# Output projection by Strassen's seven half-size products, with weight sums made in DRAM by accumulating transfers

## The chip, the cores and the metric

The kernel runs on one core of one Trainium2 chip. The metric is device time in microseconds (us) of one execution, as the median of several. PE is TensorE (its weight loads are a row of their own, PEld), DVE is VectorE, ACT is ScalarE, POOL is GpSimd, and SP is SyncE, which here only issues transfers.

## The reference

One layer of a decoder: one input projection, three branches (a gated MLP, a state-space scan, attention into 256 memory tokens), a concatenation `y` of 1024 columns, and then the part that the change rewrites:

```python
y = jnp.concatenate([y_a * jax.nn.silu(g_a), y_b * jax.nn.silu(g_b), y_x * jax.nn.silu(g_x)], axis=-1)
x = layer_norm(DN_ALPHA * x + y @ w_out[layer], ln_g[layer], ln_b[layer])
```

There are 1024 tokens, 1024 columns of `y` and 1024 columns of output, all float32; `DN_ALPHA` is the fourth root of 2.

## The kernel before

All matrix products keep float32 accuracy by three matmuls: every operand is split into a high part, rounded to the float32r that PE takes, and a low part that holds the rest. `split` (L64) makes them, a cast on ACT (L65) and a subtraction on DVE (L62), and `mm3` (L142) multiplies high by high, high by low and low by high. A tile of weights is 128 x 512: `load` (L130) brings 256 KB into one of four `raw` buffers, on SP's queue, and `piece` (L135) splits it into one of six `hi`/`lo` pairs.

The program runs through these stages, all back to back on PE: eight k-steps of the first projections (`gx`, `q`; x and its weights are loaded and split on the way; each k-step is 24 matmuls), the keys and values of the memory (`k`, `v`; pieces `wk`, `wv`, with `qs` made from `q` at the same time by `q_evac`, L256), the units `xb`, `gb`, `v`, `u`, `g` of the input projection with attention and the scan woven in, and the output projection `o`.

PE's order is the order of the code. `ordered` (L107) says whether DVE, ACT and POOL are bound to it too ("a": in the first k-steps and from the third `g` unit on) or whether a planner places their instructions ("p": between). SP's transfers are always placed by the planner. Small jobs (`spawn`, `tick`) are written into the code's order by a count of PE's time.

The output projection (L905 to L1017) goes through the 1024 output columns in two halves. In the first, eight banks of PSUM hold eight token tiles of 128, and the eight k-steps run outside, tiles inside; `o_part` (L961) adds `ALPHA * x`, which is in `res`, while it evacuates, and takes batch statistics. In the second half, tiles run outside: as one tile is complete, `finish_a` (L939) aggregates its statistics, lets POOL raise the variance to the power -1/2 (L943) and centres it on DVE (L944); `finish_b` (L947) scales on ACT (L951), adds the bias on POOL (L59) and stores it, or, for the last three tiles, does both on DVE in cuts (L957). The last tile's second half is done in two pieces of 256 columns.

Also touched: `token_bias` (L637), which starts the attention stage and has POOL fill a tile `ones` (L647) that a matmul `tb` (L650) needs.

## Time and profile before

| | |
|---|---|
| median of 3 runs | 388.81 us (388.75 to 390.43) |
| the profiled execution | 388.28 us, span 386.5 us |
| PE busy | 377.0 us, 98% of the span |
| DVE, ACT, POOL busy | 273.7, 155.6, 97.6 us |
| moved by the transfers | 37.95 MB |

The span runs from the first to the last instruction of the profiled execution. Busy times are unions over an engine's instructions, so a pipelined PE can be busy without a gap. A chain of waits is followed back from the last instruction. In a timeline, a bracket behind a row gives the idle time of the engine before it and what ended it. SPq rows are the issues of transfers by SP. Buffer numbers are left out of names.

### The profile page before, as it was taken

The numbers are of one execution on the slowest core, as the hardware profiler recorded it, in microseconds if no ns is written. First come the engines' busy times: TensorE is split into PE (matmuls) and PEld (weight loads), VectorE is DVE, ScalarE is ACT, GpSimd is POOL, SyncE is SP. The second block draws the span as 40 slices with busy tenths as digits, with TensorE's granted clock in tenths as the row PEclk, the third lists the DMA queues.
The fourth block names the chain that finished last, engine by engine and source line by source line (L and its number), as shares of the span: only waits on it lengthen the run. The fifth ranks groups of instructions, "written<-read, shape, count | busy, mean of one in ns | idle before, by whom it ended". The sixth has DMA issues, their size and how long they took to land.

```text
span 386.5 us, 5465 instructions
## 1 busy us (share of the span) xinstructions
PE 377.0 (98%) x1937; PEld 319.9 (83%) x1937; DVE 273.7 (71%) x589; ACT 155.6 (40%) x305; POOL 97.6 (25%) x77
## 2 busy tenths in 40 slices
PE   8999999999999999999999999999999999999991
PEld 7888898888888788888888888888888888888881
DVE  4689997888884999699677387958247401874476
ACT  4572696667673735131232334337136410012200
POOL 1305000000000885814927402200000000027761
PEclk9999999999999999999999999999999999999997
DMA  7973436312940123112111144000038710001224
GB/s 219 301 266 117 137 113 190 116 71 77 105 66 30 30 70 110 54 30 69 56 44 54 39 114 161 33 0 27 29 109 336 280 37 0 2 0 58 107 109 163
DMA packets 23339, 37.95 MB, mean 98 GB/s; under 512 B 5504, under 2 KB 8976, under 8 KB 23184
## 3 DMA queue, kind: packets, MB, share of 16 engines
q1 hardware_dynamic: 23312, 37.61, 31.9%
q8 instruction: 15, 0.25, 0.3%
q14 instruction: 12, 0.10, 0.1%
HBM read 31.77 MB, written 5.24 MB: 96 GB/s over the span
## 4 chain that ended last, share of the span: by engine, by line
PE 94%; issue 1%; ACT 1%; DVE 1%; DMA 1%; POOLq 0%; POOL 0%; SPq 0%; DVEq 0%
PE o L145 7%; PE o L146 7%; PE o L144 7%; PE zu L151 4%; PE zu L152 4%; PE zg L151 4%; PE zu L154 4%; PE zg L152 4%; PE zg L154 4%; PE zv L144 4%; PE zv L146 4%; PE zv L145 4%; PE av L624 2%; PE zxb L152 2%; PE zxb L154 2%; PE zxb L151 2%
## 5 line engine op out<-in xcount | busy, mean ns | idle before, releaser
L943 POOL TENSOR_TENSOR stat<-stat,nhalf 128x1 f32<-128x1 f32 x8 | 12.1, 1510 | 112.3 <-DVE stat L942 112.3
L145 PE MATMUL o<-l_wo,yh 128*128 128x512 f32 (+1 forms) x100 | 38.4, 384 | 0.0
L144 PE MATMUL o<-h_wo,yh 128*128 128x512 f32 (+1 forms) x100 | 38.3, 383 | 0.0
L146 PE MATMUL o<-h_wo,yl 128*128 128x512 f32 (+1 forms) x100 | 38.3, 383 | 0.0
L144 PE MATMUL zv<-h_v,xh 128*128 128x512 f32 x64 | 25.6, 400 | 0.3 <-ACT yb L229 0.3
L151 PE MATMUL zu<-xh,h_u 128*128 128x512 f32 x64 | 25.9, 404 | 0.0
L151 PE MATMUL zg<-xh,h_g 128*128 128x512 f32 x64 | 25.5, 398 | 0.0
L152 PE MATMUL zu<-xl,h_u 128*128 128x512 f32 x64 | 25.0, 391 | 0.0
L152 PE MATMUL zg<-xl,h_g 128*128 128x512 f32 x64 | 25.0, 390 | 0.0
L146 PE MATMUL zv<-h_v,xl 128*128 128x512 f32 x64 | 24.9, 390 | 0.0
L145 PE MATMUL zv<-l_v,xh 128*128 128x512 f32 x64 | 24.9, 389 | 0.0
L962 DVE SCALAR_TENSOR_TENSOR res<-res,o 128x512 f32<-128x512 f32 (+1 forms) x16 | 10.3, 646 | 19.0 <-PE o L146 19.0
L144 PEld LDWEIGHTS o<-h_wo,yh 128*128 128x128 f32 x100 | 18.8, 188 | 3.9
L145 PEld LDWEIGHTS o<-l_wo,yh 128*128 128x128 f32 x100 | 18.8, 188 | 3.9
L146 PEld LDWEIGHTS o<-h_wo,yl 128*128 128x128 f32 x100 | 18.8, 188 | 3.8
L62 DVE TENSOR_TENSOR l_v<-r_v,h_v 128x512 fp32r<-128x512 f32 x16 | 15.6, 978 | 7.2 <-ACT h_v L65 7.1
L65 ACT CAST h_v<-r_v 128x512 fp32r<-128x512 f32 x16 | 9.9, 620 | 26.4 <-PE zu L152 18.4
L951 ACT ACTIVATE res<-res,stat 128x1024 f32<-128x1024 f32 x5 | 5.8, 1152 | 36.6 <-POOL stat L943 36.6
L154 PE MATMUL zu<-xh,l_u 128*128 128x512 f32 x64 | 19.8, 390 | 0.0
L154 PE MATMUL zg<-xh,l_g 128*128 128x512 f32 x64 | 19.7, 389 | 0.0
L596 ACT ACTIVATE pr<-s,nm 128x256 f32<-128x256 f32 x32 | 14.9, 472 | 7.9 <-DVE nm L592 6.5
L62 DVE TENSOR_TENSOR l_wo<-r_wo,h_wo 128x512 fp32r<-128x512 f32 x12 | 8.0, 689 | 14.0 <-ACT h_wo L65 13.9
(296 smaller groups left out, 1068.6 us busy)
## 6 DMA issues: line engine op xcount, KB each, us to landing
r_v<-in_w_v_dram SPq DMA_DIRECT2D x16, 256.0 KB, 2.8
r_wo<-in_w_o_dram SPq DMA_DIRECT2D x16, 256.0 KB, 2.9
res<-in_x_dram SPq DMA_DIRECT2D x8, 512.0 KB, 6.6
r_x<-in_xT_dram SPq DMA_DIRECT2D x15, 256.0 KB, 4.8
out_dram<-res SPq DMA_DIRECT2D x6, 512.0 KB, 2.6
r_u<-in_w_fm_dram SPq DMA_DIRECT2D x8, 256.0 KB, 2.7
r_g<-in_w_fm_dram SPq DMA_DIRECT2D x8, 256.0 KB, 2.7
r_wgq<-in_w_gq_dram SPq DMA_DIRECT2D x7, 256.0 KB, 4.9
```

The source lines that it names most:

```text
L62: eng.tensor_tensor(o, a, b, op=ALU.subtract)
L65: S.copy(hi, src)
L144: T.matmul(ps, lhsT=sh, rhs=mh, start=start, stop=False, **kw)
L145: T.matmul(ps, lhsT=sh, rhs=ml, start=False, stop=False, **kw)
L146: T.matmul(ps, lhsT=sl, rhs=mh, start=False, stop=stop, **kw)
L151: T.matmul(ps[h], lhsT=wh, rhs=xh[:, kt, half[h]], start=first, stop=False, **kw[h])
L152: T.matmul(ps[h], lhsT=wh, rhs=xl[:, kt, half[h]], start=False, stop=False, **kw[h])
L154: T.matmul(ps[h], lhsT=wl, rhs=xh[:, kt, half[h]], start=False, stop=last, **kw[h])
L596: S.activation(pr[:, h], ps3[:, h], AF.Exp, bias=nm[:, h:h + 1], scale=1.0, accum_out=rs[:, h:h + 1])
L624: T.matmul(ps[:, h * 256:h * 256 + 256], lhsT=vs[:, m, 2 * hp + h], rhs=pp[:, h * 2 + m], start=h + m + n == 0, stop=h + m + n == 3, skip_ ...
L943: G.tensor_tensor(rs, rs, nhalf[:, 0:1], op=ALU.pow)
L962: V.scalar_tensor_tensor(res[:, t, c0:c0 + w], res[:, t, c0:c0 + w], ALPHA, ps[:, :w], op0=ALU.mult, op1=ALU.add)
```

## The change

The 1024 x 1024 x 1024 product becomes seven products of 512 x 512 x 512 after Strassen, in Winograd's form. Tokens are cut in halves h1 and h2, the columns of `y` in the halves (`yx`, `yb`) and `ya`, and the weights in quarters a11, a12, a21, a22. Four weight sums s1 to s4 are tensors in DRAM: SP copies a quarter into each, and POOL's queue adds the others by accumulating transfers. When they are loaded like other weights, twelve of the pieces (of s2, s4 and s3) get their low part differently: ACT casts the high part and writes its negative as the low part, and an accumulating transfer from DRAM adds the weights to it. Operands of `y` that are sums (T1 to T4) are made on DVE and then split; four of them are made in place in `yx` and `yb`.

Products run in the order of the code's list of weights (a11, s1, s2, s4, s3, a22, a12), five of them with the four k-steps outside and four token tiles inside, and the last two, T4 times a22 and B21 times a12, tile by tile. Products that share a sum stay in the same PSUM banks (`ub`, `zb`) and are evacuated in between. Layer norm no longer takes batch statistics, except for the last tile: the evacuations also add up their rows, ACT squares with the mean as bias and adds up (`means`), POOL takes the power (`deviations`), DVE centres, and `finish` scales and adds.

```diff
+    def weight_sums():
+        yield 4.0
+        nc.sync.dma_start(out=wsum["s1"], in_=quarter["a21"])
+        nc.sync.dma_start(out=wsum["s3"], in_=quarter["a21"])
+        yield 16.0
+        G.dma_start(out=wsum["s1"], in_=quarter["a22"], accum_op=ALU.add)
+        G.dma_start(out=wsum["s3"], in_=quarter["a11"], accum_op=ALU.add)
+        nc.sync.dma_start(out=wsum["s2"], in_=quarter["a11"])
+        yield 16.0
+        G.dma_start(out=wsum["s2"], in_=wsum["s1"], accum_op=ALU.add,
+                      max_dma_last_dim=8192)
+        nc.sync.dma_start(out=wsum["s4"], in_=quarter["a12"])
+        yield 16.0
+        G.dma_start(out=wsum["s4"], in_=wsum["s2"], accum_op=ALU.add,
+                      max_dma_last_dim=8192)
+
     spawn(token_bias())
+    spawn(weight_sums())
...
+    def differences(k):
+
+        b12, b11 = src1(k)[:, h2], src1(k)[:, h1]
+        sub(V, b12, ya[:, k, h2], b12)
+        V.scalar_tensor_tensor(b11, b11, -1.0, b12, op0=ALU.mult, op1=ALU.subtract)
...
+                if 8 <= i < 20:
+                    S.copy(hi, self.raws[i])
+                    S.activation(lo, hi.bitcast(F32), AF.Copy, scale=-1.0)
+                    G.dma_start(out=lo, in_=self.src(i), accum_op=ALU.add)
+                else:
+                    split(hi, lo, self.raws[i])
...
+    wo = Weights(("a11", "s1", "s2", "s4", "s3", "a22", "a12"))
...
+    def means(t0, n):
+        i = slice(at(t0), at(t0) + n)
+        V.tensor_tensor(nmean[:, i], sums[:, i, 0], sums[:, i, 1], op=ALU.add)
+        V.tensor_scalar(nmean[:, i], nmean[:, i], -1.0 / 1024, None, op0=ALU.mult)
+        for t in range(t0, t0 + n):
+            junk = gm.tile([P, 1024], BF16, tag="mt", bufs=2, name=f"junk{t}")
+            i1 = slice(at(t), at(t) + 1)
+            S.activation(junk, res[:, t], AF.Square, bias=nmean[:, i1], scale=1.0,
+                         accum_out=ssq[:, i1])
+
+    def deviations(t0, n):
+        i = slice(at(t0), at(t0) + n)
+        V.tensor_scalar(rsd[:, i], ssq[:, i], 1.0 / 1024, LN_EPS, op0=ALU.mult, op1=ALU.add)
+        G.tensor_tensor(rsd[:, i], rsd[:, i], nhalf[:, 0:n], op=ALU.pow)
...
+    def finish(t, cuts=None):
+        rs = rsd[:, at(t):at(t) + 1]
         ot = res[:, t]
-        if t < 5:
+        if cuts is None:
             S.activation(ot, ot, AF.Copy, scale=rs)
             add(G, ot, ot, lnb2)
             nc.sync.dma_start(out=out[tok[t]], in_=ot)
             return
...
+    def product(p, n, ps, start, done):
+        for k in range(4):
+            wo.fetch(4 * p + k + 5)
+            for j in range(4):
+                omm(ps[j], n, k, 4 * p + k, j, start and k == 0, k == 3)
+                if k == 3:
+                    done(j)
+                tick(0.68)
...
+    product(0, "B11", ub, True, lambda j: first(j, 0, ub[j], 1))
+    product(1, "T1", zb, True, lambda j: first(4 + j, 1, zb[j], -1))
+    product(2, "T2", ub, False, lambda j: first(4 + j, 0, ub[j], 1))
+    product(3, "B22", zb, False, lambda j: more(4 + j, 0, zb[j], 1, True))
+
+    def t2_done(j):
+        more(4 + j, 1, ub[j], -1, True)
+        if j < 2:
+            means(4 + j, 1)
+
+    product(4, "T3", ub, False, t2_done)
+    drain()
+    wo.fetch(28)
+    means(6, 2)
+    deviations(4, 2)
...
+    def last(j):
+        p2(j)
+        more(j, 0, z2[j], 1, True)
+        means(j, 1)
+
+    p4(0)
+    centre(4)
+    first(0, 1, ub[0], -1, True)
+    deviations(6, 2)
+    centre(5)
+    last(0)
+    finish(4)
+    centre(6)
+    deviations(0, 1)
+    centre(0)
+    p4(1)
+    first(1, 1, ub[1], -1, True)
+    finish(5)
+    last(1)
+    finish(0)
+    centre(7)
+    deviations(1, 1)
+    centre(1)
+    p4(2)
+    first(2, 1, ub[2], -1, True)
+    finish(6, (0, 1024))
+    last(2)
+    finish(1)
+    finish(7, (0, 1024))
+    deviations(2, 1)
+    centre(2)
+    p4(3)
+    first(3, 1, ub[3], -1)
+    V.bn_stats(bst[:, 0], res[:, 3, half[1]])
+    finish(2)
```

Three places show how instructions stand now. First SP's queue at the end of the first k-steps' loads; `ws` are the four sums, `gluw` a parameter, and the `r_m`, `r_wgq` and `r_x` behind them are the loads for the last k-step. The piece of the difference:

```order
 L639 DMA gluw<-in_glu_w_dram 128x512
+L664 DMA ws_s_819<-in_w_o_dram 128x2048
+L665 DMA ws_s_821<-in_w_o_dram 128x2048
+L669 DMA ws_s_820<-in_w_o_dram 128x2048
+L673 DMA ws_s_822<-in_w_o_dram 128x2048
 L132 DMA r_m_520<-in_memT_dram 128x512
 L132 DMA r_wgq_524<-in_w_gq_dram 128x512
```

The planner has put all four copies ahead of the last k-step's loads, long before the stage in which the code asks for them. On POOL, the four accumulating transfers stand behind the power `rr` (L417) and a fill, and ahead of the fill of `ones`.

Second, DVE in the stage of keys and values, before:

```order
L62 TENSOR_TENSOR l_wv_622<-r_wv_619,h_wv_621 128x512
L62 TENSOR_TENSOR l_wk_685<-r_wk_682,h_wk_684 128x512
L264 SCALAR_TENSOR_TENSOR qs<-q_161,qs 64x512 x2
L264 SCALAR_TENSOR_TENSOR qs<-q_162,qs 64x512 x2
L62 TENSOR_TENSOR l_wv_691<-r_wv_688,h_wv_690 128x512
L264 SCALAR_TENSOR_TENSOR qs<-q_163,qs 64x512 x2
L264 SCALAR_TENSOR_TENSOR qs<-q_164,qs 64x512 x2
```

And now, at the same place:

```order
L62 TENSOR_TENSOR l_wv_622<-r_wv_619,h_wv_621 128x512
L264 SCALAR_TENSOR_TENSOR qs<-q_161,qs 64x512 x2
L264 SCALAR_TENSOR_TENSOR qs<-q_162,qs 64x512 x2
L264 SCALAR_TENSOR_TENSOR qs<-q_163,qs 64x512 x2
L264 SCALAR_TENSOR_TENSOR qs<-q_164,qs 64x512 x2
L62 TENSOR_TENSOR l_wk_685<-r_wk_682,h_wk_684 128x512
L62 TENSOR_TENSOR l_wv_691<-r_wv_688,h_wv_690 128x512
```

The low parts of the third pair of pieces (`l_wk_685`, `l_wv_691`) moved behind all of `qs`; on ACT their casts moved behind its `qs` and a table load in the same way.

Third, POOL's last instructions now; `stat` rows are powers of the variance, `res` rows whole-tile adds of the bias:

```order
L1046 TENSOR_TENSOR stat<-stat,nhalf 128x2 x2
L59 TENSOR_TENSOR res<-res,lnp 128x1024
L1046 TENSOR_TENSOR stat<-stat,nhalf 128x1
L59 TENSOR_TENSOR res<-res,lnp 128x1024 x2
L1046 TENSOR_TENSOR stat<-stat,nhalf 128x1
L59 TENSOR_TENSOR res<-res,lnp 128x1024
L1046 TENSOR_TENSOR stat<-stat,nhalf 128x1
L59 TENSOR_TENSOR res<-res,lnp 128x1024
L1202 TENSOR_TENSOR stat<-stat,nhalf 128x1
```

In before, adds and powers alternate and the last two powers follow each other; now tile 2's add stands directly ahead of the last tile's power.

## Rows read from the trace of the kernel before

**Rows 1.** The page: busy us and share of the span; shares of the chain.

```profile
PE 377.0 (98%) x1937; PEld 319.9 (83%) x1937; DVE 273.7 (71%) x589; ACT 155.6 (40%) x305; POOL 97.6 (25%) x77
...
PE 94%; issue 1%; ACT 1%; DVE 1%; DMA 1%; POOLq 0%; POOL 0%; SPq 0%; DVEq 0%
```

**Rows 2.** Timeline of PE: start us, us, engine, line, operation, out<-in; output projection's ends.

```profile
289.92 0.40 PE L144 MATMUL o<-h_wo,yh 128*128 128x512 f32 x1
...
378.18 0.28 PE L146 MATMUL o<-h_wo,yl 128*128 128x256 f32 x1
```

**Rows 3.** Groups of PE by form, 289.8 to 378.6: count | busy us, mean ns.

```profile
L145 PE MATMUL o<-l_wo,yh 128*128 128x512 f32 x92 | 36.1, 392 | 0.0
...
L145 PE MATMUL o<-wb_l,yh 128*128 128x512 f32 x28 | 11.0, 392 | 0.0
L145 PE MATMUL o<-l_wo,yh 128*128 128x256 f32 x8 | 2.3, 282 | 0.0
```

**Rows 4.** Timeline of DVE, its last row.

```profile
382.06 1.54 DVE L957 SCALAR_TENSOR_TENSOR res<-res,stat,lnp 128x480 f32<-128x480 f32 x3 [0.44 <-POOL stat L943]
```

**Rows 5.** Timeline of POOL near the end: an add, and the last power.

```profile
365.22 2.40 POOL L59 TENSOR_TENSOR res<-res,lnp 128x1024 f32<-128x1024 f32 x1
...
380.50 1.52 POOL L943 TENSOR_TENSOR stat<-stat,nhalf 128x1 f32<-128x1 f32 x1 [4.25 <-DVE stat L942]
```

**Rows 6.** The page: a group of splits; a transfer's KB and us to landing.

```profile
L62 DVE TENSOR_TENSOR l_wo<-r_wo,h_wo 128x512 fp32r<-128x512 f32 x12 | 8.0, 689 | 14.0 <-ACT h_wo L65 13.9
...
r_wo<-in_w_o_dram SPq DMA_DIRECT2D x16, 256.0 KB, 2.9
```

**Rows 7.** Timeline of ACT: the scale of a whole tile.

```profile
365.28 1.15 ACT L951 ACTIVATE res<-res,stat 128x1024 f32<-128x1024 f32 x1 [4.35 <-POOL stat L943]
```

**Rows 8.** Timeline of SP: issues at the end of the first k-steps' loads.

```profile
23.43 0.33 SPq L639 DMA_DIRECT2D gluw<-in_glu_w_dram  x1
...
27.93 0.93 SPq L132 DMA_DIRECT2D r_x<-in_xT_dram  x2
```

**Rows 9.** Windows: load phase; loads of x and weights; a store of a tile.

```profile
23.00:26.00 3.00, 3.00 (x15) 2.49 (x14) 2.51 (x14) 2.28 (x4) 0.46 (x1) 1.00 1.00 353
26.00:28.00 2.00, 2.00 (x11) 1.65 (x10) 1.99 (x4) 1.91 (x4) 0.00 (x0) 1.00 0.26 92
...
300.00:304.00 4.00, 4.00 (x19) 3.23 (x18) 0.00 (x0) 0.50 (x1) 0.00 (x0) 1.00 1.03 403
352.00:353.25 1.25, 1.25 (x7) 1.05 (x6) 1.18 (x4) 0.00 (x0) 0.52 (x1) 1.00 1.01 413
```

**Rows 10.** Timeline of PE: eighth k-step's first matmul, third wk piece's, the ones'.

```profile
43.34 0.39 PE L151 MATMUL gx<-xh,h_wgq 128*128 128x512 f32 x1
...
54.48 0.28 PE L144 MATMUL k<-mh,h_wk 128*128 128x256 f32 x1
...
70.72 1.02 PE L650 MATMUL tb<-wT,ones 128*128 128x512 f32 x2
```

**Rows 11.** Timeline of DVE: eighth k-step's last two splits; the first of two qs runs.

```profile
40.46 1.28 DVE L62 TENSOR_TENSOR xl<-r_x,xh 128x512 fp32r<-128x512 f32 x2
...
49.78 2.80 DVE L264 SCALAR_TENSOR_TENSOR qs<-q,qs 64x512 fp32r<-64x512 f32 x4 [0.23 <-ACT qs L261]
```

**Rows 12.** Timeline of POOL between 22 and 66 us.

```profile
29.10 5.44 POOL L417 TENSOR_TENSOR rr<-et,EE 128x32 f32<-128x32 f32 x1 [5.64 <-DVE th L56]
...
60.51 0.21 POOL L647 MEMSET ones<- 128x128 f32 x1 [25.90 <-ACT h_xb L65]
```

**Rows 13.** Timeline of ACT: the table load behind qs.

```profile
53.95 1.28 ACT L237 ACT_TABLE_LOAD   x1
```

**Rows 14.** Windows behind PE's end; the granted clock is the third number from the end.

```profile
379.00:381.00 2.00, 0.00 (x0) 0.00 (x0) 1.90 (x6) 0.00 (x0) 0.50 (x1) 1.00 0.79 297
381.00:382.00 1.00, 0.00 (x0) 0.00 (x0) 0.62 (x1) 0.00 (x0) 1.00 (x1) 0.68 0.00 0
```

**Rows 15.** Timeline of PE at the start: the warm-up matmuls.

```profile
1.08 3.17 PE L243 MATMUL warm<-warm 128*128 128x128 bf16 x28 [1.08 <-DVE warm L240]
```

More of the change, by code (lines that the diff above doesn't have):

```diff
@@ L906, in trunk_kernel @@
     yp1_st, yp1 = open_pool("yp1", side="right")
[L907 to L919 removed]
+    h1, h2 = half
@@ new lines, in src1, with block, ysplit @@
+    def src1(k):
+        return (yx if k < 2 else yb)[:, k % 2]
+    ops = {}
+    def block(n, k, pool, tag):
+        t = [pool.tile([P, 512], F32R, tag=f"{tag}{x}", bufs=8 if tag == "y1" else 7, name=f"{n}{x}{k}") for x in "hl"]
+        ops[n, k] = t
+        return t
+    def ysplit(n, k, src, pool, tag):
+        split(*block(n, k, pool, tag), src)
+    def early_split():
+        for k in range(4):
+            ysplit("B11", k, src1(k)[:, h1], yp1, "y1")
+            yield 2.0
+        for k in range(4):
+            t = gm.tile([P, 512], F32, tag="mt", bufs=2, name=f"T1f{k}")
+            sub(V, t, src1(k)[:, h1], src1(k)[:, h2])
+            ysplit("T1", k, t, yp1, "y1")
+            yield 3.0
+        for k in range(3):
+            while k not in have_y:
+                yield 1.0
+            differences(k)
+            yield 2.0
@@ L1008, in trunk_kernel, with first @@
-    for c in range(2):
-        ps = zbank(f"o17{c}")
-        for i in range(KT):
-            wh, wl = wo1[i]
-            omm(ps[:, :256], 7, i, wh[:, c * 256:c * 256 + 256], wl[:, c * 256:c * 256 + 256])
-        o_part(7, 512 + c * 256, 256, ps, 2 + c)
-        if c == 0:
-            finish_b(6)
-    finish_a(7, 4)
-    finish_b(7)
+    def first(t, c, ps, sign, total=False):
+        r = res[:, t, half[c]]
+        kw = dict(accum_out=sums[:, at(t), c:c + 1]) if total else {}
+        V.scalar_tensor_tensor(r, r, ALPHA, ps, op0=ALU.mult,
+                               op1=ALU.add if sign > 0 else ALU.subtract, **kw)
@@ new lines, in more, with yprep @@
+    def more(t, c, ps, sign, total=False, cols=(0, 512)):
+        a, b = cols
+        r = res[:, t, 512 * c + a:512 * c + b]
+        kw = dict(accum_out=sums[:, at(t), c:c + 1]) if total else {}
+        V.scalar_tensor_tensor(r, ps[:, a:b], float(sign), r, op0=ALU.mult, op1=ALU.add, **kw)
+    ub = [ubank(f"o1{j}") for j in range(4)]
+    zb = [zbank(f"o5{j}") for j in range(4)]
+    def yprep():
+        differences(3)
+        for k in range(4):
+            ysplit("T2", k, src1(k)[:, h1], yp, "y2")
+            yield 2.0
+        for k in range(3):
+            ysplit("B22", k, ya[:, k, h2], yp, "y2")
+            yield 2.0
+        yield 2.0
+        for k in range(4):
+            ysplit("T3", k, src1(k)[:, h2], yp1, "y1")
+            yield 2.0
+        yield 3.0
+        ysplit("B22", 3, ya[:, 3, h2], yp, "y2")
+        yield 2.0
+        for k in range(4):
+            t4 = src1(k)[:, h1]
+            V.scalar_tensor_tensor(t4, t4, -1.0, ya[:, k, h1], op0=ALU.mult, op1=ALU.subtract)
+            ysplit("T4", k, t4, yp1, "y1")
+            yield 2.0
+        for k in range(4):
+            ysplit("B21", k, ya[:, k, h1], yp, "y2")
+            yield 2.0
@@ new lines, in omm @@
+    def omm(ps, n, k, w, j, start, stop, cols=(0, 512)):
+        wh, wl = wo.pcs[w]
+        a, b = cols
+        yh, yl = ops[n, k]
+        mm3(ps[:, a:b], yh[:, tok[j]], yl[:, tok[j]], wh[:, a:b], wl[:, a:b], start, stop, chk=True)
+    def product(p, n, ps, start, done):
+        for k in range(4):
+            wo.fetch(4 * p + k + 5)
[4 more added lines that the diff above has]
+                tick(0.68)
@@ new lines, in p2 @@
+    def p2(j, first=True, cols=(0, 512)):
+        for k in range(4):
+            omm(z2[j], "B21", k, 24 + k, j, first and k == 0, k == 3, cols)
+    def last(j):
[17 more added lines that the diff above has]
+    finish(0)
@@ new lines, in trunk_kernel @@
+    centre(7)
[13 more added lines that the diff above has]
+    finish(2)
+    for c, cols in enumerate(((0, 256), (256, 512))):
+        p2(3, c == 0, cols)
+        more(3, 0, z2[3], 1, False, cols)
+        V.bn_stats(bst[:, 1 + c], res[:, 3, cols[0]:cols[1]])
```

133 lines of the change are left out of this document (63 added, 70 removed).

## The prediction

> **What bounds the kernel now.** I read the busy shares and the chain that ended last first: TensorE (PE) is busy 98% of the span and carries 94% of the chain [rows 1]. So PE work that goes is worth its full length, and so is any wait put on PE. Then the stage that the change rewrites: its first matmul starts at 289.92 and its last ends at 378.18 + 0.28 = 378.46 [rows 2], 88.5 us without a hole. Grouped by form, one of the three lines of mm3 holds 92 + 28 matmuls of 512 columns and 8 of 256 [rows 3], its row for the other weights 8 more, and the other two lines hold the same: 360 whole ones and 48 halves, worth 384 whole ones, 0.2305 us each. Third, what follows PE: VectorE's last cut ends at 382.06 + 1.54 = 383.60 [rows 4], 5.1 us after PE; in between, GpSimd's power for the last tile runs from 380.50 to 382.02 [rows 5]. Last, the load phase, since the change puts transfers there.
>
> **Part 1, the matmuls: 11.1 us less.** Seven products of 4 k-steps, 4 token tiles and 3 matmuls are 336. Of the twelve for the last tile each is done in two halves, so 324 whole ones and 24 halves run, worth 336. At 0.2305 that is 77.4 us against 88.5. PE must find everything ready for that. Weight sums that are subtracted by an accumulating transfer are asked for four k-steps (4 x 12 x 0.23 = 11 us) ahead, of which two casts take 1.2; a 256 KB load lands in 2.9 us [rows 6]. No accumulating transfer is in this trace; up to 9 us each it costs nothing, and I price it at nothing. The sums and splits of the activations add, with the 29 evacuations, some 35 VectorE instructions of 0.69 [rows 6], about 24 us, less 15 batch statistics; VectorE is idle from 300 to 304, in the old stage [rows 9], and the operands are made one product (11 us) before their use. Nothing, too.
>
> **Part 2, the end of the kernel: 7.2 us more.** GpSimd does five whole-tile adds (2.40 us each) and a power per tile (1.52 us) [rows 5], and in before they alternate in one tile's period. Now nine of them stand in the last 22 us of PE's work, in the order that the change shows. I worked the queues forward from the end of the fifth product (call it zero) with durations of rows. ScalarE takes two whole-tile squares (1.15 each, as its whole-tile scale [rows 7]) ahead of the four casts of the last weight pieces, so VectorE has their four low parts done at 4.7 and then centres tiles 4 and 5 (1.2 each, by the 1.28 of two 512-column splits [rows 11]); the first finished sum of tile 0 is evacuated at 9.6, its square is done at 11.2, and only then does ScalarE scale tile 4, which stands behind it in its queue. GpSimd's first add starts at 12.4. From there GpSimd is one serial chain: add, power, add, add, power, (1.3 us in which ScalarE scales tile 1), add, power, (1.3 for tile 2), add, and the power of the last tile: 5 x 2.4 + 4 x 1.5 + 2.6 = 20.6, so that power ends at 33.0. VectorE's three cuts (1.54) end at 34.6. PE's last matmul ends at 22.3 (0.2 of it a wait for low parts). The distance is 12.3 instead of 5.1: 7.2 us. Ends: 2.5 if tile 4's scale finds its way as soon as tile 4 is centred (first add 4.7 earlier), 9 if squares that also add up take 0.3 more each and VectorE's summing forms 0.2 more. I take the sum as worked.
>
> **Part 3, the start: four 1 MB copies on SP's queue, 0.3 us.** They stand right behind gluw (issued at 23.43) and ahead of the loads for the eighth k-step (the last of them from 27.93) [rows 8]. The transfers have drained their backlog by 26 (353 GB/s until then, 92 after) [rows 9]. A copy from memory to memory is not in this trace. Reading runs at 403 GB/s at share 1.03, writing at 413 at share 1.01 [rows 9]. Upper rate: both go on at once at 408; 4.19 MB take 10.3 us, the four blocked loads (1.05 MB) 2.6, and all have landed at 38.9. PE takes that k-step up at 43.34 [rows 10]; the last half must land one split earlier (0.64, half of the pair's 1.28 [rows 11]), at 42.7. But GpSimd's queue issues the accumulating transfers once the power at 29.10 + 5.44 = 34.5 is over [rows 12]. If two streams that both have work get half the engines each, what is left at 35 (3.9 us) takes 7.8, landing at 42.8 and, with some 0.2 to land, a wait of 0.3. Ends: none; or, if reading and writing share the 408, copies until 46.5, left at 35 14.1 us, doubled: 63, a wait of 20. I take 0.3, because each direction alone keeps the engines at share 1.0, so the engine and not the memory is what a row shows as full.
> By the Trainium skill, "HBM Reference", Specifications, memory gives about 716 GB/s to a pair of cores; as an estimate a copy then does at most 358, ends 1.4 us later, and by the same halving the wait is some 3 us instead of 0.3 and the result 388.8. No run here shows it.
>
> **Part 4, the stage after the load phase: 0.8 us.** VectorE and ScalarE now finish all of qs before they split the third pair of kv weights. ScalarE's eight scalings end about when its table load starts (53.95; 1.28 long) [rows 13], so the cast that stood ahead of them lands near 55; PE wants it at 54.48 [rows 10]. VectorE needs two runs of 2.80 from 49.78 [rows 11], 55.4, and 0.69 more. PE waits about 0.8. Ends: 0, if ScalarE starts sooner by the cast that left, and 2.5, if the two xb casts, now both ahead of kh, wait for their load.
>
> **The sum.** This execution took 388.28 (span 386.5 and 1.8 around it); the median of the runs is 0.5 above it. 388.28 - 11.1 + 7.2 + 0.3 + 0.8 = 385.5, and 386.0 against the median of 388.81. About 0.5% (386.9 to 390.75) is what a measurement of this kernel can tell from no change.
>
> **Rivals.**
> *The copies hold up the eighth k-step* (the other side). For it: nothing in before copies memory to memory, and SP's queue is one line, so everything behind waits. Against: the load phase has share 0.26 right after [rows 9], and the two directions run at 408 each. If reading and writing share that rate, even with no halving the copies end at 46.5, the loads land at 49.4, and PE waits 6.7. A stopped PE also loses its clock: after its end at 378.46 the granted clock is 1.00 until 381, 0.68 from 381 to 382 [rows 14], on its way from the higher of its two levels (2.4 GHz) to the lower (1.2). Climbing back has a price too: the 28 warm-up matmuls of 128 columns take 3.17 us [rows 15], 0.113 each, twice 0.2305/4, so 1.6 of the 3.17 are lost at the lower level. With 1.6: 386.0 - 0.3 + 6.7 + 1.6 = 394.0. With halving as well it would be over 400. It decides from a wait of 3.4 us on: 385.7 + 3.4 + 1.6 is 390.7, slower by 0.5%.
> The Trainium skill, "DMA: Bandwidth & Descriptors", Issuing engines are not separate DMA queues, says that transfers issued by GpSimd and SP run on the same engines and interleave. By that rule the halving is real and this rival gains; the trace of before has one busy queue and cannot show it.
> *The accumulating transfers are slow.* GpSimd waits for s1's sum to issue s2's, and for s2's to issue s4's; behind them stands the fill of ones (60.51 in before [rows 12]), which PE needs at 70.72 [rows 10]. From 34.5 on two of them have 36 us: 18 each. At 24 each PE would wait 12, for 398. Against: 1 MB read twice is 5.1 us at 408.
> *The end stays short.* If GpSimd's adds find their inputs early, part 2 gives little: 386.0 - 7.2 = 378.8. Against: the order of ScalarE's queue.
> *It doesn't do what it says:* a planner moves the sums to where they are needed, and there is no saving. The order shows 336 matmuls on PE, so hardly.
>
> **How the numbers follow.** Forecast (own range 383.5 to 388.5): 0.47, of which 0.35 lies below 386.9. The end stays short: 0.15. A somewhat longer wait at the start, up to 3.4 us (up to 390.7): 0.10. The copies hold up PE for longer: 0.19. Slow accumulation: 0.08. No saving: 0.01. So faster 0.50, same 0.22, slower 0.28. The range 380.5 to 396 leaves out part of the short end and the worst of the copies, together under 2 in 10.
>
> **What would show it.** Right: in the stage PE without a hole for about 77 us; about 12 us from PE's last matmul to VectorE's last cut, with GpSimd's add and power back to back before it; PE's idle time near 43 us under 1. Wrong: PE waiting near 43 us for a VectorE split of x whose release is a transfer, with the granted clock falling; PE waiting at the ones; or GpSimd idle before the last power, which would mean that part 2 is mis-sized.

## The result, and the profile after

The changed kernel takes 406.62 us (median of 4 runs, 405.85 to 407.49) where the kernel before takes 388.78 on the same chip: a ratio of 1.0451, 95% interval 1.0414 to 1.0487. I had predicted 386.0 and a range of 380.5 to 396.0. It is 4.5% slower, and outside the range.

The page of the changed kernel, the lines that answer to [rows 1] and [rows 6] (a transfer's KB, then us from issue to landing):

```profile
PE 372.0 (92%) x1877; PEld 312.6 (77%) x1877; DVE 293.5 (72%) x629; ACT 185.9 (46%) x355; POOL 108.6 (27%) x91
...
PE 71%; DMA 11%; DVE 7%; ACT 6%; issue 2%; POOL 1%; SPq 1%; POOLq 0%; DVEq 0%; ACTq 0%
...
ws_s<-in_w_o_dram SPq DMA_DIRECT2D x4, 1024.0 KB, 11.2
```

PE has 5 us less to do, but the span is 404.8 instead of 386.5, and PE is on 71% of the chain instead of 94%. A transfer holds 11% of the chain, and before it was 1%. The next two fences show where: windows of the load phase (the columns as in [rows 9]: length, then busy us of PE, PEld, DVE, ACT and POOL, granted clock, share of the DMA engines, GB/s), and PE's waits in the whole trace.

```profile
26.00:36.00 10.00, 10.00 (x46) 8.29 (x45) 9.39 (x28) 3.10 (x5) 6.89 (x4) 1.00 1.01 351
36.00:44.00 8.00, 7.73 (x35) 6.05 (x33) 3.31 (x6) 2.56 (x4) 0.46 (x1) 1.00 0.97 233
44.00:50.00 6.00, 0.00 (x0) 0.00 (x0) 0.69 (x1) 0.62 (x1) 0.81 (x1) 0.87 1.02 223
50.00:60.00 10.00, 1.52 (x2) 0.58 (x2) 1.39 (x2) 1.63 (x3) 0.00 (x0) 0.50 1.01 256
60.00:70.00 10.00, 9.72 (x39) 7.91 (x40) 8.99 (x30) 7.64 (x15) 0.81 (x1) 0.73 0.87 203
```

```profile
PE gx L151 <- ACT xh L65: 15.0, 2, 13.9
...
PE o L144 <- DVE res L1075: 7.2, 1, 7.2
```

PE stands still from 43.7 to 57.6, at the eighth k-step, and its clock falls from the higher level (2.4 GHz, 1.00) to the lower (1.2, 0.50) and is back only after 64. Meanwhile the DMA engines are full (share 0.97 to 1.02), but from 36 on they move 223 to 256 GB/s, not 351 as from 26 to 36. Here are the issues on SP's queue (compare [rows 8]) and then on POOL's:

```profile
24.41 0.62 SPq L664 DMA_DIRECT2D ws_s<-in_w_o_dram  x1
...
26.44 1.39 SPq L673 DMA_DIRECT2D ws_s<-in_w_o_dram  x1
...
29.08 0.91 SPq L132 DMA_DIRECT2D r_x<-in_xT_dram  x2
```

```profile
34.55 1.06 POOL L667 DMA_DIRECT2D ws_s<-in_w_o_dram  x1
35.32 1.14 POOL L668 DMA_DIRECT2D ws_s<-in_w_o_dram  x1
48.32 0.81 POOL L671 DMA_DIRECT2D ws_s<-ws_s  x1 [11.86 <-DMA ws_s<-in_w_o_dram]
60.44 0.81 POOL L675 DMA_DIRECT2D ws_s<-ws_s  x1 [11.31 <-DMA ws_s<-ws_s]
```

The copies were issued from 24.4 and land one after the other, the last 15.1 us after its issue, at 41.5. The two accumulating transfers are issued at 35, but up to 40 all but 0.02 of the 0.98 MB that move from 36 on are still SP's. From then on, until the loads that PE wants have landed, the engines are mostly GpSimd's. The two queues from 44 to 48 (q0 is GpSimd's, q1 SP's; packets, MB, share of the engines' time):

```profile
q0 software_dynamic: 103, 0.71, 86.5%
q1 hardware_dynamic: 103, 0.19, 15.4%
```

The output projection, on PE (compare [rows 2]): its first matmul, the last of the fifth product, the first behind the wait of 7.2 us, and the last. Then VectorE and GpSimd at the end (compare [rows 4, 5]):

```profile
309.82 0.40 PE L144 MATMUL o<-h_wo,B11h 128*128 128x512 f32 x1
...
365.22 0.40 PE L146 MATMUL o<-h_wo,T3l 128*128 128x512 f32 x1
...
393.68 0.58 PE L144 MATMUL o<-h_wo,B21h 128*128 128x256 f32 x1 [7.20 <-DVE res L1075]
...
396.20 0.41 PE L146 MATMUL o<-h_wo,B21l 128*128 128x256 f32 x1
```

```profile
381.85 3.10 DVE L1049 SCALAR_TENSOR_TENSOR res<-res,stat,lnp 128x1024 f32<-128x1024 f32 x1
...
385.48 2.80 DVE L1061 SCALAR_TENSOR_TENSOR res<-res,stat,lnp 128x1024 f32<-128x1024 f32 x1
...
389.18 1.28 DVE L1061 SCALAR_TENSOR_TENSOR res<-res,stat,lnp 128x1024 f32<-128x1024 f32 x1
...
399.83 1.54 DVE L1061 SCALAR_TENSOR_TENSOR res<-res,stat,lnp 128x480 f32<-128x480 f32 x3 [0.44 <-POOL stat L1202]
```

```profile
380.69 6.50 POOL L59 TENSOR_TENSOR res<-res,lnp 128x1024 f32<-128x1024 f32 x2
...
395.96 2.35 POOL L59 TENSOR_TENSOR res<-res,lnp 128x1024 f32<-128x1024 f32 x1 [1.26 <-ACT res L1056]
398.26 1.53 POOL L1202 TENSOR_TENSOR stat<-stat,nhalf 128x1 f32<-128x1 f32 x1
```

So the difference of the two spans, 18.3 us, splits at two places. The stage begins at 309.82 instead of 289.92: 19.9 lost ahead of it. Of these, 19.2 are lost by the end of the eighth k-step: the first `k` matmul starts at 67.99 instead of 48.78. From there to VectorE's last cut it takes 401.37 - 309.82 = 91.55 us instead of 383.60 - 289.92 = 93.68: 2.1 gained. Another 0.5 is lost behind the last cut.

### The profile page after: what moved, and what is told of

Read it like the earlier page. It is cut to its first block, busy times and chain, and to the rows that moved or that the text cites. A ratio compares the mean times of both kernels' runs of the same rounds, so it can differ in the third digit from the quotient of the medians.

```text
span 404.8 us, 5528 instructions
## 1 busy us (share of the span) xinstructions
PE 372.0 (92%) x1877; PEld 312.6 (77%) x1877; DVE 293.5 (72%) x629; ACT 185.9 (46%) x355; POOL 108.6 (27%) x91
## 4 chain that ended last, share of the span: by engine, by line
PE 71%; DMA 11%; DVE 7%; ACT 6%; issue 2%; POOL 1%; SPq 1%; POOLq 0%; DVEq 0%; ACTq 0%
DMA r_x<-in_xT_dram 11%; PE o L145 4%; PE o L144 4%; PE o L146 4%; PE zu L151 4%; PE zu L152 4%; PE zg L151 4%; PE zu L154 4%; PE zg L152 4%; PE zg L154 4%; PE zv L144 4%; PE zv L146 3%; PE zv L145 3%; ACT junk L1040 2%; PE av L624 2%; PE zxb L152 2%
## 5 line engine op out<-in xcount | busy, mean ns | idle before, releaser
L1005 POOL DMA_DIRECT2D l_wo<-ws_s x12 | 10.4, 866 | 79.4 <-ACT l_wo L1004 76.5
L151 PE MATMUL gx<-xh,h_wgq 128*128 128x512 f32 x28 | 12.2, 435 | 15.0 <-ACT xh L65 15.0
L65 ACT CAST h_v<-r_v 128x512 fp32r<-128x512 f32 x16 | 9.9, 620 | 26.3 <-PE zu L152 18.3
L151 PEld LDWEIGHTS gx<-xh,h_wgq 128*128 128x128 f32 x28 | 5.8, 205 | 17.1 <-ACT xh L65 16.0
L705 POOL MEMSET M<- 128x512 f32 x2 | 1.0, 529 | 66.7 <-PE zgb L152 66.7
L62 DVE TENSOR_TENSOR xl<-r_x,xh 128x512 fp32r<-128x512 f32 (+1 forms) x17 | 11.0, 657 | 7.8 <-ACT xh L65 7.0
L59 POOL TENSOR_TENSOR res<-res,lnp 128x1024 f32<-128x1024 f32 x5 | 13.8, 2777 | 7.2 <-ACT res L1056 7.2
L887 DVE TENSOR_SCALAR nv<-nv,mv,rsv 128x128 f32<-128x128 f32 x32 | 13.3, 486 | 3.0 <-POOL rsv L881 3.0
L1040 ACT ACTIVATE junk<-res,stat 128x1024 bf16<-128x1024 f32 x7 | 8.0, 1146 | 16.2 <-DVE stat L1036 14.9
L144 PEld LDWEIGHTS zv<-h_v,xh 128*128 128x128 f32 x64 | 12.0, 188 | 3.0 <-ACT yb L229 0.7
L144 PE MATMUL o<-h_wo,B21h 128*128 128x512 f32 (+1 forms) x20 | 7.6, 382 | 7.2 <-DVE res L1075 7.2
```

The source lines that it names most:

```text
L59: eng.tensor_tensor(o, a, b, op=ALU.add)
L62: eng.tensor_tensor(o, a, b, op=ALU.subtract)
L144: T.matmul(ps, lhsT=sh, rhs=mh, start=start, stop=False, **kw)
L151: T.matmul(ps[h], lhsT=wh, rhs=xh[:, kt, half[h]], start=first, stop=False, **kw[h])
L887: V.tensor_scalar(sl, sl, mv[:, i, 0:1], rs[:, i:i + 1], op0=ALU.subtract, op1=ALU.mult)
L1005: G.dma_start(out=lo, in_=self.src(i), accum_op=ALU.add)
```

## Experiments

The theory after the first look (FRONT): everything that was lost was lost at the eighth k-step and the low clock behind it, and the rest of the change is worth its 2 us. The rival (END): the wait of 7.2 us in the last tile is what costs. All times below stand against runs of before on the same chip, 388.67 to 389.28 us; "ahead of `o`" is how much later than 289.92 the output projection starts.

**All transfers later.** The copies go behind the loads of `gb` pieces, the accumulating transfers behind `ones`. `spl[0]` is SP's latest load; s3, s2 and s4 follow in the same form, 8 us apart.

```diff
+    def copy_sum(n, q):
+        with tc.issue_after(spl[0].ins):
+            nc.sync.dma_start(out=wsum[n], in_=quarter[q])
...
-        yield 4.0
-        nc.sync.dma_start(out=wsum["s1"], in_=quarter["a21"])
...
+        yield 20.0
+        copy_sum("s1", "a21")
```

> The four copies and the four accumulating transfers all start behind the loads of the load phase (the copies behind loads of gb pieces on SP's queue, the accumulating ones behind the fill of ones on GpSimd's). Theory FRONT: the whole loss is the wait for the eighth k-step of x near 43 us and the low clock behind it; in the changed kernel every later stage stands 19.8 to 19.9 us later than in before (xd 76.19 to 96.10, X 97.69 to 117.47). Then 406.6 - 19.9 = 386.7 (386.0 to 388.5), PE's first o matmul comes about 20 us earlier, and PE waits under 1 us near 43. Rival END: the 7.2 us for which PE waits for VectorE in the last tile is what made the kernel slow; then the time stays above 395. If the transfers only move their harm to where they now stand, PE waits near 60 to 90 for pieces and the time lies between the two.

Measured: 399.08 us, ratio 1.0242 (1.0219 to 1.0266). The first wait is gone without a rest: `ones` is filled at 60.55 (60.51 in before). But the harm moved, as the last sentence of the expectation has it. A wait of PE in the attention, the rows of ScalarE and VectorE that lead to it, and the windows around it:

```profile
PE pt L609 <- DVE pr L604: 8.8, 2, 8.5
```

```profile
85.05 0.62 ACT L65 CAST h_gb<-r_gb 128x512 fp32r<-128x512 f32 x1 [10.96 <-DMA r_gb<-in_w_fm_dram]
```

```profile
85.70 0.69 DVE L62 TENSOR_TENSOR l_gb<-r_gb,h_gb 128x512 fp32r<-128x512 f32 x1 [9.01 <-ACT h_gb L65]
```

```profile
70.00:80.00 10.00, 8.15 (x41) 5.85 (x39) 4.98 (x14) 2.23 (x8) 0.81 (x1) 1.00 1.05 260
80.00:90.00 10.00, 2.40 (x10) 2.33 (x11) 3.65 (x10) 4.38 (x13) 0.81 (x1) 0.66 1.02 262
```

The load of the last `gb` piece was issued at 64.53, behind three of the copies, and landed 20.4 us later. PE has no use for that piece yet, but its cast and its split stand in the queues of ScalarE and VectorE, and what the attention needs stands behind them. The loads for the attention's bias (`lnb`, `bs`) come late as well and cost PE 0.7. In all 12.7 us are lost ahead of `o`, here instead of at 43. So it is not the place of the copies alone that does harm; it is any load that some queue waits for while these 8.4 MB pass.

**The copies as they were, the sums later.** This takes GpSimd's part away from the first wait. `filled[0]` is the fill of `ones`; s3's sum moves in the same way, and the other two behind it.

```diff
-        G.dma_start(out=wsum["s1"], in_=quarter["a22"], accum_op=ALU.add)
+        with tc.issue_after(filled[0].ins):
+            G.dma_start(out=wsum["s1"], in_=quarter["a22"], accum_op=ALU.add)
```

> The four copies stay where the change put them, ahead of the eighth k-step's loads on SP's queue; only GpSimd's four accumulating transfers move, behind the fill of ones. Theory SUMS: between 26 and 36 us, with the copies alone, the engines moved 315 to 393 GB/s, so the copies were nearly through at 36.5, and only the accumulating transfers (issued at 34.55 and 35.32; from 36 on 209 to 262 GB/s at share 0.9 to 1.1) kept the 1.05 MB of loads behind them from landing. Then the loads land by 40, PE doesn't wait near 43, and the time is that of the run with all transfers late, 386.7 (386 to 389). Theory COPIES (the rival of the prediction): a copy's reading and writing share one rate, the copies end at 46.5 and the loads land at 49.4: a PE wait of 6.7 and 1.6 of clock, 395, or more.

Measured: 397.87 us, ratio 1.0217 (1.0155 to 1.0278). By the total neither theory holds, since the sums do harm again where they now stand (PE is busy 6.51 of the 10 us from 80). By the place the question is answered; windows, and the fill of `ones`:

```profile
26.00:36.00 10.00, 10.00 (x45) 8.27 (x45) 9.12 (x31) 3.16 (x5) 5.53 (x2) 1.00 0.98 349
36.00:44.00 8.00, 7.95 (x34) 5.85 (x32) 4.68 (x8) 3.29 (x5) 0.00 (x0) 1.00 0.92 245
44.00:50.00 6.00, 3.90 (x10) 2.34 (x10) 4.14 (x14) 4.18 (x7) 0.00 (x0) 0.85 0.60 196
```

```profile
65.99 0.21 POOL L649 MEMSET ones<- 128x128 f32 x1 [30.56 <-PE v L146]
```

The copies alone move 349 GB/s until 36 and 245 from there to 44, so that drop is not the sums' doing. PE waits about 2 us, and with the lower clock 5.5 us are lost by the first `k` matmul and by `ones`. In the changed kernel `ones` stands at 80.42, 19.9 late. Here the planner has also put the splits of the third pair of pieces back where they stood in before, which is worth 0.7 (see part 4 below). So of 19.9 us the copies make 5.5, the accumulating transfers 13.7 and that order 0.7, by one profiled execution each.

**What of the accumulating transfers does it: their rows, or the adding?** Three kernels leave everything where the change put it: rows of 2 KB instead of 8; plain copies instead of adding; and both. The first edit, for s1's sum:

```diff
-        G.dma_start(out=wsum["s1"], in_=quarter["a22"], accum_op=ALU.add)
...
+        G.dma_start(out=wsum["s1"], in_=quarter["a22"], accum_op=ALU.add,
+                      max_dma_last_dim=2048)
```

> Everything stands where the change put it, but the accumulating transfers go in rows of 2 KB instead of 8 KB. Theory TURNS: each engine takes a row from GpSimd's queue and a row from SP's in turn, so with rows of 8 KB against the loads' 2 KB the loads get a fifth of what moves (1.05 MB from 36 to 58 are 48 of some 230 GB/s). With equal rows they get half, 115 GB/s: 9 us from 36.5, landing at 46, a PE wait of about 3 and 1 to 2 of clock: 391 (388 to 396). Theory HALVES (equal time for each queue whatever the rows, and the accumulating transfers slow by themselves): nothing changes, 405 to 408, or more if four times the rows cost GpSimd time.

> GpSimd's four early transfers are plain copies of the same bytes, rows and queue, without adding (the weight sums are left out, so the output projection multiplies wrong weights; its amount of work is the same). Theory ADDING: an accumulating transfer reads two things for each that it writes and so holds the engines about twice as long (in the changed kernel's trace GpSimd's queue moved 4.19 MB in 34.6% of 60 us, 202 GB/s of its own time; SP's 10.71 MB in 55.2%, 323). Plain, the first two are through by 44 and the loads land near 45: PE waits about 2 and loses 1 of clock, 390 (387.5 to 394). If the adding costs nothing and only a second queue's presence does harm: 403 to 407.

> GpSimd's four early transfers are plain copies and go in rows of 2 KB: both changes of the two runs with one of them each (the weight sums are left out, so the output projection multiplies wrong weights; its amount of work is the same). The fill of ones stood at 60.51 in before, 65.99 with the copies alone in front, 73.43 with plain transfers of 8 KB rows, 74.05 with adding ones of 2 KB rows and 80.42 as the change has it. If rows and adding are two causes that act apart, each takes off some 7 of the 14.4 us that GpSimd's transfers cost, and both together leave 1 to 4: ones at 67 to 70, time 393 to 396.5. If it is one cause (the engines' time that the transfers take, whichever way), the second change gives little: ones at 72 to 74, time 399 to 401.

| GpSimd's transfers | time (ratio) | PE's wait for `xh` | lost ahead of `o` | SP's part of the bytes |
|---|---|---|---|---|
| adding, packets of 8 KB (the change) | 406.62 (1.0451) | 15.0 | 19.9 | 0.19 of 0.90 MB |
| adding, 2 KB | 403.42 (1.0359) | 4.1 | 17.0 | 0.86 of 1.81 MB |
| plain, 8 KB | 400.09 (1.0274) | 6.5 | 12.9 | 0.32 of 1.61 MB |
| plain, both edits: 4 KB | 400.28 (1.0292) | 7.5 | 12.3 | 0.69 of 2.14 MB |

The last column is SP's queue in a stretch in which both queues have work: 44 to 48, 46 to 53, 42 to 47 and 43 to 49. GpSimd's queue between 20 and 120 us, in the order of the table (64 of the packets have 4 bytes; the others carry the 4.19 MB):

```profile
q0 software_dynamic: 576, 4.19, 20.7%
```

```profile
q0 software_dynamic: 2112, 4.19, 23.0%
```

```profile
q0 software_dynamic: 576, 4.19, 11.4%
```

```profile
q0 software_dynamic: 1088, 4.19, 11.7%
```

The counts show that both edits together did not give rows of 2 KB: 1024 packets for 4.19 MB are 4 KB each.

The same 4.19 MB take 20.7 us of all sixteen engines when they add and 11.4 when they don't: 202 GB/s against 368. That is theory ADDING, and it is worth 7.0 of the 19.9 us. The price I had expected for the plain run (390) was still far too low: PE waited 6.5, not 2.

Rows are another matter. Both queues in the run with adding rows of 2 KB, from 46 to 53:

```profile
q0 software_dynamic: 480, 0.95, 73.1%
q1 hardware_dynamic: 474, 0.86, 37.8%
```

While both queues have work, they are served packet for packet: 480 to 474 here, 103 to 103 in the changed kernel, 173 to 174 in the plain run from 42 to 47 and 374 to 380 with both edits from 43 to 49 (the short ones counted in; without them 87 to 93 in the changed kernel). The loads' packets are of 2 KB, so beside packets of 8, 4 and 2 KB they get about 1/5, 1/3 and 1/2 of the bytes, as the table has it. That is theory TURNS, and its mechanism holds; its price (391) does not. With adding, short rows let the loads through sooner (15.0 to 4.1), but the sums then run longer, the next pieces (`wk`, `wv`) wait, and 17.0 of 19.9 us are lost all the same. Without adding, both edits together gain nothing over one: ScalarE casts the last half of x at 52.80 in the plain run and at 52.16 with both, so a larger share of the bytes did not bring it much sooner.

**All transfers in a calm stretch.** The copies go behind `v` and `g` pieces, the sums follow, from about 178 to 240 us: the job starts with the `v` unit, its first copy 85 us later, the others 10 us apart.

```diff
-    spawn(weight_sums())
     gate[0] = now[0] + 4.0
...
+    spawn(weight_sums())
     run_units([v_units[0], *us, v_units[1], gs_[0], gs_[1]], gs_[2])
```

> The four copies and four accumulating transfers run in a stretch in which the trace of before shows the DMA engines at 37 to 54 GB/s: the copies behind v and g pieces on SP's queue (from about 178 us), the accumulating transfers on GpSimd's from about 188 to 240. Nothing of them is left in the load phase and the attention. Theory FRONT: 406.6 - 19.9 = 386.7 (385.5 to 388.5): the matmuls' saving and the longer end as predicted, and nothing else. If the accumulating transfers slow pieces wherever they stand, PE waits for a piece between 180 and 250 and the time is 388.5 to 393.

Measured: 387.36 us, ratio 0.9959 (0.9945 to 0.9972). PE's one long wait, its timeline at the stage's start and at the end of the fifth product, and VectorE's last row:

```profile
PE o L146 <- DVE res L1084: 7.2, 1, 7.2
```

```profile
290.61 0.40 PE L146 MATMUL o<-h_wo,B11h 128*128 128x512 f32 x1
...
346.18 0.39 PE L148 MATMUL o<-h_wo,T3l 128*128 128x512 f32 x1
```

```profile
380.79 1.54 DVE L1070 SCALAR_TENSOR_TENSOR res<-res,stat,lnp 128x480 f32<-128x480 f32 x3 [0.44 <-POOL stat L1211]
```

FRONT holds, to 0.7 us. The same 8.4 MB cost PE nothing between 178 and 240: the stage starts 0.7 later than in before instead of 19.9, and these 0.7 are there at the first `k` matmul (49.45, 48.78 in before), long ahead of the transfers. The splits of the third pair of pieces stand here as in before, so part 4 of the prediction has gone too. From the end of the fifth product (346.57) to the last cut (382.33) it takes 35.76, and in the changed kernel 401.37 - 365.62 = 35.75: the end is the same, with all of its waits. So END is not what made the kernel slow.

**A bank for the last tile's second half.** On top of the run before, as for all that follow.

```diff
     for c, cols in enumerate(((0, 256), (256, 512))):
-        p2(3, c == 0, cols)
+        if c:
+            z2[3] = zbank("o2x")
+        p2(3, True, cols)
```

> As the run with the transfers at 178 to 240, and the last tile's second half gets a PSUM bank of its own, as in before, so that its matmuls needn't wait for VectorE to read the first half (PE's one wait of 7.2 us in the output projection). Theory CHAIN: GpSimd's chain (add, power, add, power) sets the end; the last power starts when the add before it is over, so taking away PE's wait leaves the time within 0.6 us of the other run. Rival WAIT: those 7.2 us lie on the path, and 4 to 7 us are gained.

Measured: 386.52 us, ratio 0.9937 (0.9919 to 0.9955). PE's last matmul and VectorE's last cut:

```profile
368.26 0.28 PE L148 MATMUL o2x<-h_wo,B21l 128*128 128x256 f32 x1
```

```profile
379.92 1.54 DVE L1070 SCALAR_TENSOR_TENSOR res<-res,stat,lnp 128x480 f32<-128x480 f32 x3 [2.74 <-POOL stat L1213]
```

PE's wait of 7.2 us was worth 0.8, close to the 0.6 that CHAIN allowed and far from the 4 to 7 of the rival. PE now ends some 9 us sooner, and VectorE's idle time ahead of its last cuts grew from 0.44 to 2.74, released by GpSimd's power. CHAIN holds.

**The fifth product tile by tile.** Four kernels; the last three mend what the one before them showed. Behind each tile's `means` stand the power, the centring and the finish of the tiles before it.

```diff
-    product(4, "T3", ub, False, t2_done)
+    wo.fetch(22)
+    for j in range(4):
+        for k in range(4):
+            omm(ub[j], "T3", k, 16 + k, j, False, k == 3)
+            tick(0.68)
+        more(4 + j, 1, ub[j], -1, True)
+        means(4 + j, 1)
...
```

> As the run with the bank of its own, and the fifth product goes tile by tile instead of k-step by k-step, so that the sums of tiles 4 to 7 end 2.8, 5.5, 8.3 and 11.1 us after its start instead of all between 9 and 11.1; their squares, powers and adds follow tile by tile, and tiles 6 and 7 go by ScalarE and GpSimd instead of VectorE's cut. Theory CHAIN: GpSimd's adds start some 6 us earlier, and from the end of the fifth product to VectorE's last cut it takes 30 to 32 us instead of 35.9 (seven adds and five powers on GpSimd, of which about two adds and three powers lie ahead of the end of that product): 3.5 to 6 us less than the run with the bank, 381 to 383.5. Rival VECTORE: VectorE is the bound there (9.7 of 10 us busy between 380 and 390 in the changed kernel), and less than 1.5 us is gained.

> As the run with the fifth product tile by tile, with what made PE wait there mended: pieces are fetched one k-step earlier in the fourth product, the fifth's last two low parts are made by VectorE instead of an accumulating transfer, the last products' pieces are split while the fifth's last tile runs instead of behind it, and tile 2 is finished by VectorE, so that the last power on GpSimd doesn't stand behind an add. Theory PIECES: the run before lost to PE's waits for pieces (2.0, 1.3, 0.3, 2.7 and 1.1 us in its output projection, and the lower clock behind them: 0.67 from 340 to 350, 0.84 and 0.82 from 350 to 370), not to the order of the tiles. Without them PE needs 22.1 us from the end of the fifth product to its last matmul, and the last cut ends 5 to 6.5 later instead of 13: against 386.5 of the run with the bank some 6 to 7 less, 379.5 (378.5 to 382), 2% faster than before. Rival ORDER: four pieces needed at once can't be had with six buffers, PE goes on waiting, and the time stays above 385.

> As the run before it, but the two pieces that have buffers of their own are 22 and 23 instead of 24 and 25, so that all four pieces of the sixth product can be split before the fifth begins, and the last four during its last tile. Theory PIECES: there PE's waits (3.1, 2.0, 1.7 and smaller, 8.5 us in all, and a clock of 0.86 and 0.63 from 350 to 370) came from pieces 22 to 27, loaded and split behind the fifth product. They go, and with them 8 to 12 us of 392.9: 381 to 385, below the run with the bank (386.5). Rival ORDER: another engine's queue takes the place of these waits, and the time stays above 386.

> As the fifth product tile by tile with buffers of their own for pieces 22 and 23, and the last four pieces' splits stand ahead of the squares and scales on ScalarE and of the centring on VectorE, and ahead of GpSimd's adds, beside which a split of one piece took 2.45 us instead of 0.69. Theory QUEUE: what was left of PE's waits (1.2, 2.9, 2.0 and a clock of 0.71 from 360 to 370) came from pieces 24 to 27 that stood behind the finishing of tiles 4 and 5 in ScalarE's and VectorE's queues. Then 391.0 falls by 6 to 10: 381 to 385. Rival PORT: VectorE's work beside GpSimd's adds is what is full, the waits move to the sums of tiles 0 and 1, and it stays above 387.

Measured: 397.22, 392.94, 391.04 and 388.58 us, ratios 1.0197, 1.0106, 1.0060 and 0.9984 (0.9959 to 1.0010). None of the four betters the run with a bank of its own. The first three lost to PE's waits for pieces (7.4, 8.5 and 7.5 us in the output projection, with a lower clock behind them): a product that goes tile by tile wants four pieces at once, and six buffers hold them only if casts, splits and loads stand in the right order in four queues. In the third, PE, VectorE and GpSimd at one such wait:

```profile
357.48 0.51 PE L146 MATMUL o<-h_wo,B21h 128*128 128x512 f32 x1 [2.95 <-ACT h_wo L65]
```

```profile
357.46 2.45 DVE L62 TENSOR_TENSOR l_wo<-r_wo,h_wo 128x512 fp32r<-128x512 f32 x1 [1.66 <-ACT h_wo L65]
```

```profile
357.00 2.36 POOL L59 TENSOR_TENSOR res<-res,lnp 128x1024 f32<-128x1024 f32 x1 [0.79 <-ACT res L1065]
```

The split of one piece takes 2.45 us beside GpSimd's add, 0.69 otherwise [rows 6]. In the fourth, PE waits for next to nothing any more (0.9 us in all), and the end still isn't earlier. PE's first and last matmul of the stage, and VectorE's last row:

```profile
292.20 0.40 PE L146 MATMUL o<-h_wo,B11h 128*128 128x512 f32 x1
...
371.27 0.28 PE L148 MATMUL o2x<-h_wo,B21l 128*128 128x256 f32 x1
```

```profile
380.56 2.73 DVE L1070 SCALAR_TENSOR_TENSOR res<-res,stat,lnp 128x1024 f32<-128x1024 f32 x4
```

From the first matmul to VectorE's end the stage takes 383.29 - 292.20 = 91.09 us, and in the run with a bank 381.46 - 290.36 = 91.10: nothing gained, nothing lost. The 1.8 us by which this execution began the stage later were lost ahead of its first `q` matmul (10.2, and 8.4 in the run with a bank), where nothing was changed. VectorE ends 11.7 us behind PE: the theories of pieces and queues were right about PE, and the rival PORT about the time. Its reason, that tiles that end earlier only put GpSimd's adds beside more of VectorE's work, fits the trace (two centrings take 4.62 us there beside an add), but this run does not separate it from VectorE's own work.

**Without GpSimd's adds, and without the last of them.** The first leaves the five adds out, and with them the bias of five tiles; the second has VectorE finish tile 2 (the `finish` lines).

```diff
-            add(G, ot, ot, lnb2)
...
-    finish(2)
...
+    finish(2, (0, 1024))
     finish(3, (0, 480, 832, 1024))
```

> As the run with the bank of its own, without GpSimd's five whole-tile adds (the last bias is left out of tiles 0, 1, 2, 4 and 5, so their output lacks it). In that run VectorE's last cut starts at 379.92, 11.4 us after PE's last matmul ended at 368.54, and waits 2.74 for GpSimd's power, which stands behind an add. Theory GPSIMD: without the adds the powers follow VectorE at once, VectorE's work beside them takes its own time (1.28 us for a whole tile, where 3.10 and 2.80 stood beside adds; some 5 us of such stretching in all), and the last cut ends 5 to 6 us behind PE: 380.5 to 382.5 instead of 386.5. Rival VECTORE: VectorE's own work is what is full; then less than 2 us is gained.

> As the run with the bank of its own, and tile 2 is finished by VectorE in one whole-tile operation (1.28 us) instead of ScalarE's scale and GpSimd's add, so that the last power need not wait for that add (376.61 + 2.77 = 379.38 there, while VectorE had its input ready near 377). Theory GPSIMD: the power starts 1.5 to 2.4 us earlier, VectorE's operation fits into its wait of 2.74, and 1 to 2 us is gained: 384.5 to 385.5, about 1% faster than before. Rival VECTORE: VectorE reaches the last cuts no earlier, and the time stays at 386.2 to 387.

Measured: 380.40 us, ratio 0.9783 (0.9763 to 0.9803), and 385.79 us, ratio 0.9932 (0.9917 to 0.9946). Without the adds, PE's last matmul and VectorE's last cut:

```profile
369.27 0.28 PE L148 MATMUL o2x<-h_wo,B21l 128*128 128x256 f32 x1
```

```profile
374.37 1.54 DVE L1070 SCALAR_TENSOR_TENSOR res<-res,stat,lnp 128x480 f32<-128x480 f32 x3 [0.44 <-POOL stat L1213]
```

The distance from PE's end to the last cut falls from 12.9 us to 6.4, near the 5.1 of before: GpSimd's five adds are worth 6.1 us of time, by their chain and by what they do to VectorE (its whole-tile operations take 1.27 or 1.28 there); how much by which, no run separates. Taking only the last add off the path brings 0.7, less than the 1 to 2 expected: VectorE, stretched by the adds before it, was itself late. That kernel, with calm transfers, a bank of its own and tile 2 on VectorE, is the best complete one: 0.7% faster than before, where the change as made is 4.5% slower.

## Why the prediction was wrong

**Part 3 is the step that failed: 0.3 us forecast, 19.2 measured.** What failed is its share for the loads, "If two streams that both have work get half the engines each". From 44 to 48 SP's queue had 15.4% of the engines' time and GpSimd's 86.5%: the queues are served packet for packet, and GpSimd's packets are four times as long and add. From 44 to 57.6 the loads that PE wanted, and what stood behind them, got 0.69 of the 3.12 MB that moved, 22%. The copies' rate failed too, but less. I took 408 GB/s for each direction and all four landed at 36.3; they moved 351 at share 1.0 from 26 to 36, and the last landed at 41.5. Alone, the copies make 5.5 of the 19.2 us. And where I had 1.6 for the clock, some 4 of the 19.2 us are no wait: the eighth k-step's matmuls ran at the lower clock.

The Trainium skill's figure that I set beside it ("HBM Reference", Specifications, from which I estimated at most 358 for a copy) agrees with the mean of 351, but as a ceiling it does not hold: from 28 to 31 the copies alone moved 407.

Under "slow accumulation" I asked only whether GpSimd would reach `ones` in time, with 5.1 us for a sum. As the engines' time for one sum that was right (20.7 for four). But s1's sum took 13.5 from issue to landing (34.55 to 48.1), since nothing of it moved before 39 and it then shared the engines with s3's sum and the loads, and the harm was done to SP's loads long before `ones`. The stated upper end, a wait of 20, came nearer (15.0 measured), for a wrong reason (two directions sharing 408), and I left it out of the range as the worst of the copies.

The Trainium skill, "Collectives: The Full Stack", The bandwidth ceiling, says of the adding step of a collective that it reads two sources for each that it writes and so comes to about half the rate of a copy. These traces agree: 202 against 368 GB/s. My 5.1 us already counted two reads; the loads' share it does not tell.

**Which rival it was.** The one on the other side, "the copies hold up the eighth k-step", by its place, its falling clock and its "over 400 with halving", with a chance of 0.19 for all of it. What decided was not the copies' own rate, as it said, but the sums beside them. Of the signs that I gave, the wait near 43 and the falling clock came, with ScalarE's cast of x in the place of VectorE's split.

**Part 1 was right**: five products take 55.8 us (55.3 forecast), and in the run with a bank of its own PE is through from 290.36 to 368.54, 78.2 us, against the 77.4 and 0.2 of the text. No piece was late; the low parts made by accumulating transfers held PE up by at most 0.2 us.

**Part 2 was right in its mechanism and near in its size.** I had GpSimd's first add 12.4 us after the end of the fifth product, and it came at 12.1 (377.68); the last cut at 34.6, and it ended at 35.75. The miss of 1.2 goes with something that I did not see: VectorE's operations beside GpSimd's adds take 2.80 and 3.10 us instead of 1.28, and two adds 6.50 instead of 4.8; two of the powers, at 0.55 instead of 1.5, gave some of it back. The Trainium skill, "SBUF — State Buffer", Who interferes with whom, says that a VectorE instruction with two inputs from SBUF and a GpSimd instruction that reads there block each other. By that rule the adds cost VectorE's time too; the run without them agrees. I also overlooked that the last tile's halves share a bank. That put 7.2 us of waiting into PE's row, and cost 0.8, since GpSimd's chain was later still. It also hid the sign that I had named, 12 us from PE's last matmul to the last cut: 4.8 as the change is (401.37 - 396.61), 12.9 with a bank of its own.

**Part 4 was right**: 0.8 us forecast, 0.7 measured. In the changed kernel PE goes from the first `k` matmul to the last in 79.23 - 67.99 = 11.24 us, in before in 59.32 - 48.78 = 10.54, and the matmul that is held up is one that takes the low part of the third pair:

```profile
74.50 0.39 PE L146 MATMUL k<-mh,l_wk 128*128 128x256 f32 x1 [0.22 <-DVE l_wk L62]
```

In the runs whose transfers stand elsewhere the planner puts these splits back ahead of the second half of `qs`, and the stage takes 10.54 again (48.81 to 59.35 with all transfers later).

With 19.2 for part 3, 0.7 for part 4 and 1.2 more for part 2, the sum of the prediction is 386.0 - 0.3 + 19.2 - 0.8 + 0.7 + 1.2 = 406.0, against 406.6 measured.

## What to carry to other kernels

Price a transfer that nobody waits for by what it keeps from landing: list the loads that pass the engines in the same microseconds, and whether PE, or a queue that PE depends on, wants one of them. Two busy queues were served a packet each in turn here, so the one with the longer packets got more of the bytes. An accumulating transfer counts about double, and the planner's early slot for something that is needed 250 us later is the worst one; in a calm stretch the same bytes were free. At the end of a kernel, a long wait in PE's row is worth nothing while another engine's chain ends later; taking the suspected work out altogether tells in one run what it is worth.
